# Latents normalised by token tile straight from PSUM, latent weights prepared in the first stage

## The chip, the cores and the metric

The kernel runs on one core of one Trainium2 chip. The metric is the device time of one execution in microseconds (us). On this core TensorE (PE) does the matrix products, VectorE (DVE), ScalarE (ACT) and GpSimd (POOL) work on tiles in the on-chip memory SBUF and, except POOL, in PSUM, where matmuls leave their sums; SyncE (SP) starts the transfers from HBM.

## The reference, cut to what matters

Two layers (DEPTH 2), 512 tokens, 1024 features. In each layer the normalised input is multiplied by one wide weight w_in, whose columns feed four head groups. The change is in the part that prepares group A, latent attention: two low-rank latents, cq (256 columns) and ckv (128 columns), are normalised and then multiplied by w_uq and w_ukv.

```python
for l in range(DEPTH):
    h = _rmsnorm(x, norm_g[l])
    p = _split(h @ w_in[l])
    o_a = _mla(p["a_cq"], p["a_ckv"], p["a_krope"], mla_qa_g[l], mla_w_uq[l],
               mla_kva_g[l], mla_w_ukv[l], cos, sin)
...
def _rmsnorm(x, g):
    xf = x.astype(jnp.float32)
    y = xf * lax.rsqrt(jnp.mean(xf * xf, axis=-1, keepdims=True) + NORM_EPS)
    return (y * g.astype(jnp.float32)).astype(x.dtype)
...
def _mla(cq, ckv, krope, qa_g, w_uq, kva_g, w_ukv, cos, sin):
    q = (_rmsnorm(cq, qa_g) @ w_uq).reshape(B, S, H, MLA_NOPE + MLA_ROPE)
    kv = (_rmsnorm(ckv, kva_g) @ w_ukv).reshape(B, S, H, MLA_NOPE + MLA_V)
    k_rope = _rope(krope, cos, sin)
    ...
```

The other head groups (differential, top-k selected and convolutional) follow in the same layer; the selected group needs 40 more columns (kidx and widx) that are produced together with the latents.

## The kernel before, in words

All matrix products are done on pairs of a rounded high part and the remainder: `mm3` issues three matmuls for one product (high by high, high by low, low by high). A weight tile arrives by DMA in a slot called wr, ACT casts it into wh (L106), and POOL subtracts (L101, 256 columns an instruction) to give wl. A result in PSUM is split by ACT (L115 or L118, the high part) and DVE (L116 or L119, the low part).

A Tile scheduler chooses the order of each engine's instructions from dependences and priorities, and every engine then works through its own list in that order: an instruction that waits holds up what stands behind it. Tiles come from pools with a fixed number of slots; a tile whose slots are all in use waits until one is freed. PSUM has eight banks: three called proj, two s, two pt, one o. Raw weights have four slots (wr), the split weights four each (wh, wl).

Each layer has a **first stage**: for four token tiles t and four quarters q of w_in's rows, `first_part` accumulates 456 columns in the PSUM tile acc[t] (cq 256, ckv 128, the rotary key krope 32, kidx and widx 40). The order over (t, q) is a written table, `FIRST`. The acc tiles of t = 0, 1 are proj banks, those of t = 2, 3 are s banks. With the last quarter ACT copies all 456 columns to SBUF (t1, L517).

Then follows the **latent stage**, `latent()`, on PE merged with 'features': `feat` projections of 128 columns of w_in for other groups (24 matmuls of 128x512 each, which need a proj bank, and whose result ACT and DVE evict). In program order the latent stage is:

- `rep`, a tile with kidx repeated (L587) and widx (L591), and `rep_turn`: four PE transposes of rep into a pt bank (L523), then kst (L594, L595);
- the sums of squares on ACT (L599, L600), one reciprocal root for all four token tiles and both latents (`rsqrt`, L140 to L147: a first guess from the bits and three Newton steps, 11 DVE instructions of 128x8), eight scalings to the tile cn (L608);
- twelve PE transposes of cn in three pt banks (L616), each split to cT (L118, L119);
- the rotary key: small DVE operations (L630 to L636), `rep_turn` again, and the split L640;
- w_ukv: DMA (L648), ACT cast (L651), two POOL subtractions (L654); then two key products, evicted by `halves`, and four value products (the `V` tiles), all in proj banks;
- w_uq: DMA (L671), eight casts on ACT (L681), eight subtractions on POOL (L682), four products.

Attention units (`unit_a`, L720) follow. Lines that the rows name besides: L186 to L199 is `params()`, once in the whole kernel, with one Exp table load on ACT (L197); L280 to L288 is the norm of whole rows of x, which uses a root on ACT (Sqrt), a DVE reciprocal and one Newton step; L217 builds a bias table.

## Time and profile before

| what | value |
|---|---|
| median of 3 runs | 704.25 us (703.63 to 704.76) |
| profiled execution | 706.75 us, its span 705.0 us |
| TensorE clock, mean granted | 0.969 |
| PE busy | 637.8 us (90%) |
| DVE busy | 490.3 us (70%) |
| ACT busy | 382.3 us (54%) |
| POOL busy | 275.7 us (39%) |

The time of a run is a little longer than the span from the first to the last instruction of the profile: 1.75 us in the profiled execution. Busy shares are averages over the span; the clock is the share of TensorE's full speed that was granted. "PEld" in the rows is PE's loading of weights, which lies beside its matmuls.

### The profile page before, as it was taken

To read this page: it belongs to the slowest core of one execution; us is meant where nothing else is said; L and a number is where in the kernel's file an instruction comes from. 1 tells how busy PE (TensorE), PEld (TensorE's weight loads), DVE (VectorE), ACT (ScalarE), POOL (GpSimd) and SP (SyncE) were. 2 spreads that over 40 slices of the span, in tenths; PEclk is the share of its full clock that TensorE was granted. 3 is DMA by queue.
4 is the path that set the end of the run, shared out by engine and by line. 5 is a ranking of instruction groups with operands and counts; after the bars stand their busy time and mean duration, and the time that the engine had idled before them with its cause. 6 is when DMAs were issued, how large, how long until landed. Compare 5 with 4: busy or idle time off the path is not lost. (4 is left out here: it accounts for less than half of the span.)

```text
span 705.0 us, 11082 instructions
## 1 busy us (share of the span) xinstructions
PE 637.8 (90%) x3600; PEld 538.9 (76%) x3608; DVE 490.3 (70%) x1464; ACT 382.3 (54%) x910; POOL 275.7 (39%) x408
## 2 busy tenths in 40 slices
PE   3987999789999898999999779998999999999994
PEld 2675878678788677899978567887878986789994
DVE  4665664389999797645384846769999959664537
ACT  7673475376453455454387355866554345445435
POOL 3173333413533443343432543234353354334355
PEclk9997999899999999999999889999999999999998
DMA  7545265384457220234261653354533841023203
GB/s 226 120 119 160 64 121 136 110 177 120 101 130 218 69 82 32 70 140 113 57 195 32 181 149 94 113 145 109 129 90 91 223 113 46 22 67 143 91 1 119
DMA packets 86441, 79.67 MB, mean 113 GB/s; under 512 B 7286, under 2 KB 73400, under 8 KB 86384
## 3 DMA queue, kind: packets, MB, share of 16 engines
q1 hardware_dynamic: 86384, 78.98, 40.7%
q8 instruction: 28, 0.46, 0.3%
q14 instruction: 29, 0.24, 0.1%
HBM read 64.18 MB, written 12.16 MB: 108 GB/s over the span
## 5 line engine op out<-in xcount | busy, mean ns | idle before, releaser
L101 POOL TENSOR_TENSOR wl<-wr,wh 128x256 fp32r<-128x256 f32 (+1 forms) x304 | 224.2, 770 | 355.6 <-ACT wh L106 287.1
L127 PE MATMUL ps_proj<-big,wh 128*128 128x512 f32 x768 | 257.3, 409 | 1.3 <-DVE prob L471 1.0
L127 PE MATMUL ps_proj<-wh,big 128*128 128x256 f32 (+2 forms) x768 | 173.8, 312 | 2.1 <-DVE prob L762 1.3
L127 PEld LDWEIGHTS ps_proj<-big,wh 128*128 128x128 f32 x768 | 142.2, 194 | 26.0 <-DVE prob L471 1.4
L127 PE MATMUL ps_proj<-big,wl 128*128 128x512 f32 x384 | 153.6, 400 | 0.0
L127 PEld LDWEIGHTS ps_proj<-wh,big 128*128 128x128 f32 x768 | 129.8, 193 | 8.5 <-ACT big L118 1.6
L127 PE MATMUL ps_proj<-wl,big 128*128 128x256 f32 (+2 forms) x384 | 117.4, 306 | 1.1 <-DVE wl L108 1.0
L106 ACT CAST wh<-wr 128x1024 fp32r<-128x1024 f32 (+2 forms) x84 | 83.8, 998 | 36.5 <-PE ps_proj L127 19.9
L127 PEld LDWEIGHTS ps_proj<-big,wl 128*128 128x128 f32 x384 | 73.8, 192 | 14.6
L127 PEld LDWEIGHTS ps_proj<-wl,big 128*128 128x128 f32 x384 | 74.3, 194 | 4.8 <-DVE wl L108 2.1
L116 DVE TENSOR_TENSOR ptl<-ps_pt,pth 128x128 fp32r<-128x128 f32 (+1 forms) x96 | 46.6, 485 | 33.5 <-ACT pth L115 32.9
L115 ACT CAST pth<-ps_pt 128x128 fp32r<-128x128 f32 (+1 forms) x96 | 40.6, 425 | 46.3 <-PE ps_pt L413 45.9
L127 PE MATMUL ps_o<-pth,vt 128*128 128x256 f32 (+1 forms) x288 | 60.9, 283 | 4.7 <-ACT pth L115 3.2
L477 ACT ACTIVATE prob<-ps_s,st_a 128x128 f32<-128x128 f32 (+1 forms) x64 | 33.9, 530 | 45.1 <-DVE st_a L489 29.6
L127 PEld LDWEIGHTS ps_o<-pth,vt 128*128 128x128 f32 x288 | 49.9, 198 | 9.8 <-ACT pth L115 6.3
L413 PE MATMUL ps_pt<-ident,prob 128*128 128x128 f32 x240 | 43.2, 279 | 11.6 <-ACT prob L481 8.9
L574 DVE MATCH_REPLACE8 ia<-m,ia 128x256 f32<-128x256 f32 (+2 forms) x96 | 52.0, 545 | 0.1
L573 DVE MAX8 m<-ia 128x8 f32<-128x256 f32 (+2 forms) x96 | 50.8, 551 | 1.0 <-POOL ia L565 0.8
L127 PE MATMUL ps_o<-ptl,vt 128*128 128x256 f32 (+1 forms) x144 | 42.8, 297 | 6.0 <-DVE ptl L116 6.0
L413 PEld LDWEIGHTS ps_pt<-ident,prob 128*128 128x128 f32 x240 | 28.5, 140 | 23.8 <-ACT prob L481 14.5
L481 ACT ACTIVATE prob<-prob,st_a 128x128 f32<-128x128 f32 (+1 forms) x64 | 35.8, 564 | 10.8 <-DVE st_a L480 10.7
L115 ACT CAST vt<-ps_proj 128x128 fp32r<-128x128 f32 x48 | 12.3, 265 | 46.8 <-PE ps_proj L127 29.1
(159 smaller groups left out, 1000.2 us busy)
## 6 DMA issues: line engine op xcount, KB each, us to landing
wr<-in_w_in_dram SPq DMA_DIRECT2D x56, 512.0 KB
big<-trip SPq DMA_DIRECT2D x64, 128.0 KB
trip<-big SPq DMA_DIRECT2D x28, 256.0 KB
big<-in_x_dram SPq DMA_DIRECT2D x7, 512.0 KB
wr<-in_w_in_dram SPq DMA_DIRECT2D x8, 416.0 KB
big<-trip SPq DMA_DIRECT2D x32, 96.0 KB
wr<-in_w_out_dram SPq DMA_DIRECT2D x8, 384.0 KB
big<-big SPq DMA_DIRECT2D x8, 256.0 KB
```

What stands on the lines that cost most here:

```text
L101: nc.gpsimd.tensor_tensor(out=o[:, c], in0=a[:, c], in1=b[:, c], op=OP.subtract)
L106: nc.scalar.copy(h[:, :n], raw[:, :n])
L115: nc.scalar.copy(hi, src)
L116: nc.vector.tensor_tensor(out=lo, in0=src, in1=f(hi), op=OP.subtract)
L127: nc.tensor.matmul(o, lhsT=a, rhs=b, start=start and i == 0 and j == 0, stop=stop and i == n - 1 and j == 2, skip_group_check=skip)
L413: nc.tensor.transpose(b[:, k * P:(k + 1) * P], p[:, k * P:(k + 1) * P], ident)
L477: nc.scalar.activation(p[:, :W], s[:, :W], AF.Exp, scale=-1.0, bias=mn, accum_out=sums)
L481: nc.scalar.activation(p[:, :W], p[:, :W], AF.Copy, scale=st[:, 2:3])
L573: nc.vector.max(out=m8, in_=a)
L574: nc.vector.match_replace(out=a, in_to_replace=m8, in_values=a, imm_value=MARK)
```

## The change

Two things change in each layer. First, each token tile is normalised on its own as soon as its last quarter is in PSUM (`first_norm`): ACT takes the squares from PSUM (with the 1/n as a scale), DVE adds the epsilon, ACT takes the root, DVE the reciprocal and one Newton step, and DVE scales from PSUM straight to cn. ACT copies only the 72 columns that are not latents to t1. The reciprocal root for all tiles together is gone, and with it the copy of 456 columns. What read t1 in two halves (rep, widx and the rotary key) now does so in one instruction for all four tiles. Second, the load and the split of w_ukv stand at the head of `latent()` (`latent_weights`) and no longer behind the rotary key. Lines below this point move by 7 to 20: L523 becomes L543, L616 L633, L651 L609, L654 L612, L681 L688.

```diff
--- before.py
+++ after.py
@@ -490,8 +490,9 @@
                                            scale=1.0, scalar=far, op0=OP.add, op1=OP.min, accum_out=mn)
 
 
-        t1s = [big(FT), big(FT)]
-        t1 = lambda t, c0, c1: t1s[t // 2][:, t % 2, c0:c1]
+
+        t1 = sm.tile([P, NT, 72], FT, name="t1", bufs=1)
+        cn = [flat(big(FT)), flat(big(FT))]
 
         acc, fw = {}, {}
 
@@ -514,7 +515,26 @@
             mm3(acc[t][:, :456], [hT.k(2 * q + k, t) + (wh[:, k, :], wl[:, k, :]) for k in range(2)],
                 start=q == 0, stop=q == 3)
             if q == 3:
-                nc.scalar.copy(t1(t, 0, 456), acc[t][:, :456])
+                first_norm(t, acc[t])
+
+        def first_norm(t, a):
+
+            w = sm.tile([P, 8], FT, name="ssa")
+            m, r, u = w[:, 0:2], w[:, 2:4], w[:, 4:6]
+            jk = prob()
+            for c, (c0, c1) in enumerate(((0, 256), (256, 384))):
+                nc.scalar.activation(jk[:, c0:c1], a[:, c0:c1], AF.Square, scale=(c1 - c0) ** -0.5,
+                                     accum_out=m[:, c:c + 1])
+            nc.vector.tensor_scalar(out=m, in0=m, scalar1=EPS, scalar2=None, op0=OP.add)
+            nc.scalar.activation(r, m, AF.Sqrt)
+            nc.scalar.copy(t1[:, t], a[:, 384:456])
+            nc.vector.reciprocal(out=r, in_=r)
+            nc.vector.tensor_tensor(out=u, in0=r, in1=r, op=OP.mult)
+            nc.vector.scalar_tensor_tensor(out=u, in0=u, scalar=-0.5, in1=m, op0=OP.mult, op1=OP.mult)
+            nc.vector.scalar_tensor_tensor(out=r, in0=u, scalar=1.5, in1=r, op0=OP.add, op1=OP.mult)
+            for c, (c0, c1) in enumerate(((0, 256), (256, 384))):
+                nc.vector.tensor_scalar(out=cn[t // 2][:, (t % 2) * 512 + c0:(t % 2) * 512 + c1], in0=a[:, c0:c1],
+                                        scalar1=r[:, c:c + 1], scalar2=None, op0=OP.mult)
 
         def rep_turn(rep):
 
@@ -580,33 +600,30 @@
 
 
 
+        def latent_weights():
+            raw = raw_tile()
+            nc.sync.dma_start(raw[:, :512], w_ukv[l])
+            w = big()
+            kh, kl = w[:, 0, :], w[:, 1, :]
+            rk = raw[:, :512].rearrange("p (h b c) -> p b h c", h=4, b=2)
+            nc.scalar.copy(kh.rearrange("p (b h c) -> p b h c", h=4, b=2), rk)
+            for b in range(2):
+                c = slice(b * 256, (b + 1) * 256)
+                nc.gpsimd.tensor_tensor(out=kl[:, c].rearrange("p (h c) -> p h c", h=4), in0=rk[:, b],
+                                        in1=f(kh)[:, c].rearrange("p (h c) -> p h c", h=4), op=OP.subtract)
+            A["ukv"] = kh, kl
+
         def latent():
+            latent_weights()
             rep = prob()
             repv = rep.rearrange("p (t r c) -> p t r c", t=NT, r=4)
-            for i in range(2):
-                nc.vector.tensor_copy(repv[:, 2 * i:2 * i + 2],
-                                      t1s[i][:, :, None, 416:448].to_broadcast([P, 2, 4, 32]))
+            nc.vector.tensor_copy(repv, t1[:, :, None, 32:64].to_broadcast([P, NT, 4, 32]))
             widx = A["widx"] = sm.tile([P, NT, 8], FT, name="widx", bufs=2)
-            for i in range(2):
-                nc.vector.tensor_copy(widx[:, 2 * i:2 * i + 2], t1s[i][:, :, 448:456])
+            nc.vector.tensor_copy(widx, t1[:, :, 64:72])
             b = rep_turn(rep)
             A["kst"] = kst = pi.tile([P, S], FR, name="kst")
             nc.scalar.copy(kst, b)
             nc.vector.tensor_tensor(out=kst[64:P], in0=b[64:P], in1=f(kst)[64:P], op=OP.subtract)
-            ss = sm.tile([P, NT, 2], FT, name="ssa")
-            for t in range(NT):
-                jk = prob()
-                nc.scalar.activation(jk[:, :256], t1(t, 0, 256), AF.Square, accum_out=ss[:, t, 0:1])
-                nc.scalar.activation(jk[:, 256:384], t1(t, 256, 384), AF.Square, accum_out=ss[:, t, 1:2])
-            for c, n in ((0, 256), (1, 128)):
-                nc.vector.tensor_scalar(out=ss[:, :, c], in0=ss[:, :, c], scalar1=1.0 / n, scalar2=EPS,
-                                        op0=OP.mult, op1=OP.add)
-            ra = rsqrt(ss.rearrange("p t c -> p (t c)"), 2 * NT)
-            cn = [flat(big(FT)), flat(big(FT))]
-            for t in range(NT):
-                for c, (c0, c1) in enumerate(((0, 256), (256, 384))):
-                    nc.vector.tensor_scalar(out=cn[t // 2][:, (t % 2) * 512 + c0:(t % 2) * 512 + c1], in0=t1(t, c0, c1),
-                                            scalar1=ra[:, 2 * t + c:2 * t + c + 1], scalar2=None, op0=OP.mult)
             yield CH[0]
             cT = []
             for j in (2, 0, 1):
@@ -623,14 +640,12 @@
             r2 = rep.rearrange("p (t r c) -> p t r c", t=NT, r=4)
             ta = sm.tile([P, NT, 16], FT, name="ropa", bufs=1)
             tb = sm.tile([P, NT, 16], FT, name="ropb", bufs=1)
-            for i in range(2):
-                x1, x2 = t1s[i][:, :, 384:400], t1s[i][:, :, 400:416]
-                tt = slice(2 * i, 2 * i + 2)
-                co, si = ctok[:, tt, 0:16], ctok[:, tt, 16:32]
-                nc.vector.tensor_tensor(out=ta[:, tt], in0=x2, in1=si, op=OP.mult)
-                nc.vector.tensor_tensor(out=tb[:, tt], in0=x1, in1=si, op=OP.mult)
-                nc.vector.tensor_tensor(out=r2[:, tt, 0, 0:16], in0=x1, in1=co, op=OP.mult)
-                nc.vector.tensor_tensor(out=r2[:, tt, 0, 16:32], in0=x2, in1=co, op=OP.mult)
+            x1, x2 = t1[:, :, 0:16], t1[:, :, 16:32]
+            co, si = ctok[:, :, 0:16], ctok[:, :, 16:32]
+            nc.vector.tensor_tensor(out=ta, in0=x2, in1=si, op=OP.mult)
+            nc.vector.tensor_tensor(out=tb, in0=x1, in1=si, op=OP.mult)
+            nc.vector.tensor_tensor(out=r2[:, :, 0, 0:16], in0=x1, in1=co, op=OP.mult)
+            nc.vector.tensor_tensor(out=r2[:, :, 0, 16:32], in0=x2, in1=co, op=OP.mult)
             nc.vector.tensor_tensor(out=r2[:, :, 0, 0:16], in0=r2[:, :, 0, 0:16], in1=ta, op=OP.subtract)
             nc.vector.tensor_tensor(out=r2[:, :, 0, 16:32], in0=r2[:, :, 0, 16:32], in1=tb, op=OP.add)
             nc.vector.tensor_copy(r2[:, :, 1:4, :], r2[:, :, 0:1, :].to_broadcast([P, NT, 3, 32]))
@@ -644,15 +659,7 @@
                 nc.sync.dma_start(f(kk)[96:100], dmask[:, 1])
             yield 0.4
 
-            raw = raw_tile()
-            nc.sync.dma_start(raw[:, :512], w_ukv[l])
-            kh, kl = (w[:, i, :] for w in (big(),) for i in range(2))
-            rk = raw[:, :512].rearrange("p (h b c) -> p b h c", h=4, b=2)
-            nc.scalar.copy(kh[:, :512].rearrange("p (b h c) -> p b h c", h=4, b=2), rk)
-            for b in range(2):
-                c = slice(b * 256, (b + 1) * 256)
-                nc.gpsimd.tensor_tensor(out=kl[:, c].rearrange("p (h c) -> p h c", h=4), in0=rk[:, b],
-                                        in1=f(kh)[:, c].rearrange("p (h c) -> p h c", h=4), op=OP.subtract)
+            kh, kl = A["ukv"]
             for j in range(2):
                 o = bank("proj")
                 mm3(o, [(kh[:, j * P:(j + 1) * P], kl[:, j * P:(j + 1) * P], ckv[:, 0, :], ckv[:, 1, :])])
```

The scheduler turns this into other lists. **PE, layer 0, end of the first stage**: `ps_s` is the last accumulation, L186 the transpose of parameters, `big,wh` and `big,wl` rows are a feature's matmuls. Before:

```order
L127 MATMUL ps_s<-wh,big 128x456
L186 MATMUL ps_pt<-ident,prow 128x20
L523 MATMUL ps_pt<-ident,prob 128x128 x2
L127 MATMUL ps_proj<-big,wh 128x512 x2
L127 MATMUL ps_proj<-big,wl 128x512
L127 MATMUL ps_proj<-big,wh 128x512 x2
L127 MATMUL ps_proj<-big,wl 128x512
L127 MATMUL ps_proj<-big,wh 128x512
L523 MATMUL ps_pt<-ident,prob 128x128 x2
L127 MATMUL ps_proj<-big,wh 128x512
L127 MATMUL ps_proj<-big,wl 128x512
```

After:

```order
L127 MATMUL ps_s<-wh,big 128x456
L186 MATMUL ps_pt<-ident,prow 128x20
L127 MATMUL ps_proj<-big,wh 128x512 x2
L127 MATMUL ps_proj<-big,wl 128x512
L127 MATMUL ps_proj<-big,wh 128x512 x2
L127 MATMUL ps_proj<-big,wl 128x512
L127 MATMUL ps_proj<-big,wh 128x512 x2
L543 MATMUL ps_pt<-ident,prob 128x128 x4
L127 MATMUL ps_proj<-big,wl 128x512
L127 MATMUL ps_proj<-big,wh 128x512 x2
```

The transposes of rep stood in two pairs, the first directly behind L186 and the second five feature matmuls later; now all four stand together, behind eight feature matmuls.

**ACT, layer 0, latent stage**: `wh<-wr` are weight casts, L118 and L115 are evictions from PSUM, the L517, L599 and L600 rows above these are gone. Before, from the cast of kst:

```order
L594 CAST kst<-ps_pt 128x512
L600 ACTIVATE prob,ssa<-big 128x128
L599 ACTIVATE prob,ssa<-big 128x256
L600 ACTIVATE prob,ssa<-big 128x128
L106 CAST wh<-wr 128x1024 x2
L118 ACTIVATE big<-ps_proj 128x512
L118 ACTIVATE big<-ps_pt,pcol 128x512 x3
L115 CAST big<-ps_pt 32x1024
L106 CAST wh<-wr 128x1024
L651 CAST big<-wr 128x512
L118 ACTIVATE big<-ps_proj 128x512
L681 CAST big<-wr 128x256 x2
```

After, from the last tile's surroundings:

```order
L106 CAST wh<-wr 128x1024
L529 ACTIVATE ssa<-ssa 128x2
L609 CAST big<-wr 128x512
L625 CAST kst<-ps_pt 128x512
L106 CAST wh<-wr 128x1024
L118 ACTIVATE big<-ps_proj 128x512
L118 ACTIVATE big<-ps_pt,pcol 128x512 x3
L115 CAST big<-ps_pt 32x1024
L115 CAST big<-ps_proj 64x512
L106 CAST wh<-wr 128x1024
L115 CAST big<-ps_proj 64x512
L197 ACT_TABLE_LOAD
```

The cast of w_ukv (L651, now L609) moved from behind the evictions of cT to a place ahead of kst; the root of the last tile (L529) stands behind a weight cast; and the table load of `params()` (L197), which stood in the first stage, now stands among the evictions of the key products.

**ACT, layer 1, end of the first stage.** Before:

```order
L517 COPY big<-ps_s 128x456
L599 ACTIVATE prob,ssa<-big 128x256
L600 ACTIVATE prob,ssa<-big 128x128
L106 CAST wh<-wr 128x1024
L517 COPY big<-ps_s 128x456
L599 ACTIVATE prob,ssa<-big 128x256
L600 ACTIVATE prob,ssa<-big 128x128
L594 CAST kst<-ps_pt 128x512
L106 CAST wh<-wr 128x1024 x2
L118 ACTIVATE big<-ps_proj 128x512
L118 ACTIVATE big<-ps_pt,pcol 128x512 x3
```

After:

```order
L530 COPY t_4180<-ps_s 128x72
L529 ACTIVATE ssa<-ssa 128x2
L106 CAST wh<-wr 128x1024
L609 CAST big<-wr 128x512
L526 ACTIVATE prob,ssa<-ps_s 128x256
L526 ACTIVATE prob,ssa<-ps_s 128x128
L530 COPY t_4180<-ps_s 128x72
L529 ACTIVATE ssa<-ssa 128x2
L106 CAST wh<-wr 128x1024
L625 CAST kst<-ps_pt 128x512
L106 CAST wh<-wr 128x1024
L118 ACTIVATE big<-ps_proj 128x512
```

A weight cast now stands between the last tile's root and the cast of kst (L594, now L625), where kst stood ahead of both casts before.

## Rows read from the trace of the kernel before

**Rows 1.** The page's first part: busy us (share of the span) xinstructions

```profile
PE 637.8 (90%) x3600; PEld 538.9 (76%) x3608; DVE 490.3 (70%) x1464; ACT 382.3 (54%) x910; POOL 275.7 (39%) x408
```

**Rows 2.** Timeline of PE, layer 0: start, us, line, count [idle before <-releaser]

```profile
42.38 0.37 PE L127 MATMUL ps_s<-wh,big 128*128 128x456 f32 x1
...
54.96 1.12 PE L616 MATMUL ps_pt<-ident,big 128*128 128x128 f32 x4 [3.99 <-DVE big L608]
...
60.08 0.39 PE L127 MATMUL ps_proj<-big,wl 128*128 128x512 f32 x1
...
60.31 0.39 PE L127 MATMUL ps_proj<-big,wh 128*128 128x512 f32 x1
...
64.91 0.73 PE L127 MATMUL ps_proj<-big 128*128 128x512 f32 x2 [0.72 <-ACT big L651]
...
67.93 2.08 PE L127 MATMUL ps_proj<-big 128*128 128x512 f32 x4 [2.29 <-POOL big L654]
...
70.66 0.63 PE L127 MATMUL ps_proj<-big,wl 128*128 128x512 f32 x1
...
73.64 0.64 PE L127 MATMUL ps_proj<-big,wh 128*128 128x512 f32 x2
```

**Rows 3.** Timeline of PE, layer 1

```profile
397.61 0.33 PE L616 MATMUL ps_pt<-ident,big 128*128 128x128 f32 x1 [2.88 <-DVE big L608]
...
399.00 0.47 PE L616 MATMUL ps_pt<-ident,big 128*128 128x128 f32 x1 [1.06 <-DVE big L608]
...
400.41 1.79 PE L616 MATMUL ps_pt<-ident,big 128*128 128x128 f32 x6 [0.94 <-DVE big L608]
...
404.79 0.48 PE L127 MATMUL ps_proj<-big,wl 128*128 128x512 f32 x1
...
409.94 0.73 PE L127 MATMUL ps_proj<-big 128*128 128x512 f32 x2 [1.46 <-ACT big L651]
...
412.96 2.08 PE L127 MATMUL ps_proj<-big 128*128 128x512 f32 x4 [2.29 <-POOL big L654]
...
418.55 0.63 PE L127 MATMUL ps_proj<-big,wh 128*128 128x512 f32 x2
```

**Rows 4.** Windows: stretch, length, busy PE, PEld, DVE, ACT, POOL, PEclk, DMA

```profile
54.96:74.12 19.16, 16.15 (x53) 11.97 (x54) 8.98 (x17) 8.92 (x19) 7.59 (x14) 0.69 0.45 127
606.00:609.60 3.60, 3.53 (x14) 3.33 (x15) 0.38 (x3) 0.00 (x0) 0.00 (x0) 0.53 0.32 106
238.70:242.00 3.30, 3.07 (x16) 2.36 (x17) 2.21 (x9) 2.11 (x6) 0.21 (x1) 1.00 0.88 242
```

**Rows 5.** Timeline of DVE, layer 0 and then layer 1

```profile
49.15 0.66 DVE L145 TENSOR_TENSOR rs_t<-rs_y 128x8 f32<-128x8 f32 x1
...
53.95 0.17 DVE L146 SCALAR_TENSOR_TENSOR rs_t<-rs_t,ssa 128x8 f32<-128x8 f32 x1
...
396.58 4.23 DVE L608 TENSOR_SCALAR big<-big,rs_y 128x256 f32<-128x256 f32 x8
```

**Rows 6.** Timeline of POOL, layer 0

```profile
35.64 8.46 POOL L101 TENSOR_TENSOR wl<-wr,wh 128x256 fp32r<-128x256 f32 x12 [11.06 <-ACT wh L106]
48.35 5.54 POOL L101 TENSOR_TENSOR wl<-wr,wh 128x256 fp32r<-128x256 f32 x8 [4.26 <-ACT wh L106]
```

**Rows 7.** Timeline of ACT, layer 0

```profile
40.75 0.42 ACT L599 ACTIVATE prob<-big 128x256 f32<-128x256 f32 x1
...
42.11 1.28 ACT L197 ACT_TABLE_LOAD   x1
```

**Rows 8.** Groups by line and shape, ACT: busy us, mean ns

```profile
L280 ACT ACTIVATE nw<-ss 128x1 f32<-128x1 f32 x12 | 3.5, 288 | 0.1
```

**Rows 9.** Timeline of ACT, layer 1

```profile
396.24 1.04 ACT L106 CAST wh<-wr 128x1024 fp32r<-128x1024 f32 x1 [1.88 <-DMA wr<-in_w_in_dram]
```

**Rows 10.** Timeline of PE, two later waits

```profile
238.84 0.39 PE L752 MATMUL ps_s<-big 128*128 128x256 f32 x1 [2.15 <-DVE prob L762]
...
606.07 0.55 PE L127 MATMUL ps_o<-ptl,vt 128*128 128x256 f32 x1 [1.63 <-DVE ptl L116]
```

## The prediction

> **What bounds the kernel now.** I read the page first: PE is busy for 637.8 us, 90% of the span [rows 1], so what can be gained lies in the places where PE waits or runs slowly. The timeline of PE shows these around the change. In layer 0 the first stage's last matmul starts at 42.38 and ends at 42.75. Then PE stands still three times: 3.99 us before the transposes of cn, released by a scaling L608 on DVE; 0.72 before the key products, released by the cast L651; 2.29 before the next product, released by POOL's subtraction L654 [rows 2]. Layer 1 has the same three places: 2.88, 1.06 and 0.94 behind L608, 1.46 behind L651, 2.29 behind L654 [rows 3]. Sums: 7.00 and 8.63.
>
> After long waits the matmuls themselves are slower. A 128x512 matmul is followed by the next after 0.23 us at 60.08, but seven of them take 2.98 from 70.66 to 73.64, 0.43 each [rows 2]. The windows view says why: over 54.96 to 74.12 the granted clock was 0.69, and where a stretch is slow from end to end it is 0.53, the lower level of 1.2 GHz, against 1.00 at 2.4 GHz [rows 4]. In the timeline the slow stretches last from 54.96 to 60.08 and from 67.93 to 73.64, in layer 1 from 400.41 to 404.79 and from 412.96 to 418.55 [rows 2, 3]: 5.12, 5.71, 4.38 and 5.59 us. At half speed half of each is lost: 2.56, 2.86, 2.19, 2.80, together 10.4. What the two stages lose is thus 7.00 + 8.63 + 10.4 = 26.0 us.
>
> Who sets the long wait? The root of all tiles is one chain of dependent DVE instructions of 128x8. Beside POOL's subtractions they take 0.66 each, and 0.17 as soon as POOL has stopped (it worked from 48.35 to 53.89) [rows 5, 6]. The later waits are only a matter of place: w_ukv is split when ACT and POOL come to it.
>
> **The change part by part.**
>
> *The waits for L651 and L654.* The cast of w_ukv now stands ahead of kst on ACT, and POOL's two pieces follow it. They are over before the cn transposes start, since ACT has the one cast and POOL two pieces of about 0.7 (5.54 for 8) [rows 6] to do. Both waits go: 0.72 + 2.29 and 1.46 + 2.29, with the slow stretches behind them.
>
> *The wait for L608.* PE has feature matmuls from the last accumulation up to the cn transposes, before and after; it came there at 50.97 (54.96 - 3.99) [rows 2]. In the new order tiles 0 and 1 are scaled by about 46. Tile 3 is last: its root stands behind a cast of 1.04 [rows 9], then come reciprocal, three Newton operations and two scalings. If POOL subtracts meanwhile, three operations of 0.66 (2.0) instead of 0.17 (0.5) [rows 5]. I come to 52.3 to 53.2 for the last scaling. PE, which loses some time ahead of this (next part), comes there at 52.6 to 53.1. I put the wait at 0, with 1.0 as the upper bound. In layer 1 tiles 0 to 2 are finished inside the first stage, but a weight cast has moved ahead of what PE needs, and this cast can start only when its DMA has landed: at 396.24 in the trace, after 1.88 of waiting [rows 9]. From this I work out 2.75 us of waiting at the cn transposes of layer 1, between 0 and 3.9 (the sum of the last two waits there now, 1.06 + 0.94, and another 1.9).
>
> A rule of the Trainium skill speaks against small chains here: "SBUF — State Buffer", section "Who interferes with whom", says that DVE and POOL share one port pair as an exclusive lock, which a DVE instruction with two SBUF inputs needs, while one with at most one SBUF input outside certain fast modes doesn't. The 0.66 against 0.17 agree [rows 5]. By that rule the new scalings, which read PSUM, are free of POOL, whereas the scalings from SBUF took 0.53 each beside it (4.23 for 8) [rows 5]; no row here has a scaling from PSUM. Counted at 0.53 the eight cost 4.2 a layer on DVE, at an estimated 0.35 they cost 2.8; DVE has room for either except for tile 3's two, 0.4 us, which lies inside the bound of 1.0.
>
> *A new wait at the first transposes of rep (L543).* Before, half of rep was transposed early, half five matmuls later. Now all four transposes need the 72 columns of all four tiles, and behind them in PE's list stand all the feature matmuls and the cn transposes. PE gets there eight matmuls after the stage, 42.9 + 8 x 0.23 = 44.75 [rows 2]. ACT does per tile two squares, the small copy and a root of 0.29 [rows 8]. From a first square at 40.75 to the table load at 42.11, 1.36 us [rows 7], lie one such pair and one copy of 456 columns; with a copy of 72 I estimate 1.05 (0.8 and 0.25). All of it is in one queue in which a root waits for DVE's add, and that add stands on DVE behind the Newton operations of the tile before, at 0.66 each until POOL stops at 44.10 [rows 5, 6]. By this the last small copy ends at 46.3, the 512-column copy of rep on DVE 0.5 to 0.7 later, and the transposes start at 47.4: a wait of 2.6 us, with bounds of 0.9 (ACT never held up: 42.75 + 0.8 + 0.25 + 0.7 and the queue's steps, 45.65) and 3.5. In layer 1, where three tiles are done earlier, 0.9, between 0.3 and 1.5.
>
> *What was hidden under the removed waits.* Between the first cn transpose and the first value product, 54.96 to 74.12, PE has 19.16 - 0.72 - 2.29 - 5.42 = 10.7 us of work at full clock, and ACT was busy for 8.92 [rows 4]. Of this the cast L651 goes (about 0.6), and in layer 0 the table load (1.28 [rows 7]) with its two exponentials comes in: 10.0. The two engines are now of nearly the same length and take turns: an eviction on ACT waits for PE's product, a proj bank for the eviction, and behind the evictions stand the casts for the next features. Neither hides the other fully. Going through both lists row by row I get a wait of 1.3 at the third feature and 2.45 at the value products in layer 0, and 1.85 and 1.35 in layer 1 (no table load, but the late cast). Bounds: nothing, and 6 in each layer.
>
> *What costs nothing.* Fewer, larger rotary instructions; and the smaller copy, 72 instead of 456 columns. Holding the acc banks up to the scaling costs nothing in layer 0: the features that take these proj banks come 5 us later. The number of table loads stays the same.
>
> *The clock.* Whether a new wait brings the clock down isn't clear from its length: after 2.15 us at 238.84 the window is at 1.00, after 1.63 at 606.07 it is at 0.53 [rows 4, 10]. I count one fall per layer, 2.6 each (the mean of the four above, 10.4 / 4); bounds are none and two.
>
> **The sum.** New waits in layer 0: 2.6 + 0 + 1.3 + 2.45 = 6.35. In layer 1: 0.9 + 2.75 + 1.85 + 1.35 = 6.85. Clock 5.2. Gain: 26.0 - 6.35 - 6.85 - 5.2 = 7.6 us. The lists of PE behind the latent stage hold the same work, and PE is the engine that is short there, so I let the gain stand to the end. The profiled execution of 706.75 (span 705.0) would become 699.15. It is 2.5 above the median of 704.25; taken from the median, 696.6.
>
> **The rivals.**
>
> *The new waits are small (gain 13 to 21).* If ACT keeps up with PE, the waits at the proj banks go, and the clock holds. For it: ACT stood idle for over half of the stretch [rows 4], and each wait is then under 3 us. Against it: ACT's gaps are waits for PE, not room. Time with only the waits of rep and of layer 1's transposes left: 704.25 - (26.0 - 2.6 - 0.9 - 2.75) = 684.5.
>
> *The clock falls at every new wait (gain about 2).* Two falls per layer as now: 26.0 - 13.2 - 10.4 = 2.4, so 701.9. For it: a fall after 1.63 [rows 10]. Against it: the new waits are split in smaller pieces with matmuls in between.
>
> *Slower: a convoy on ACT.* A weight cast needs a free slot, which PE frees only after a whole feature, 24 x 0.23 = 5.5 us. If an eviction stands right behind such a cast and PE, further on, waits for the bank of that eviction, PE loses up to 5.5 in each layer more than counted: 13.2 + 5.2 + 11 = 29.4 against 26.0, hence 3.4 slower, 707.6. It decides from 3.8 us more per layer. For it: in both layers the first key eviction stands directly ahead of a weight cast and the others behind it. Against it: the slots are four, and now too the cast at 396.24 waited for its DMA and not for a slot [rows 9].
>
> *Nothing is left of it.* The gain at the start is given back at some later stage that DVE sets (the top-k search) or that waits for a DMA: 704. Against it: DVE's work moves forward with PE's.
>
> **How the numbers follow.** The forecast (gain 4 to 13, 691 to 700) has 0.50. Small new waits (under 691) 0.16. Clock falls everywhere (700 to 703) 0.16. No change left 0.08, the convoy 0.10. A measurement of this kernel tells a difference of about 0.2% (1.4 us) from none. Faster takes the forecast, the first rival and most of the second: 0.79. Within 0.2%: 0.10, slower 0.11. The range goes from 686, into the first rival, to 704, past the second: outside lie about 0.08 below and 0.12 above. The forecast's own range is 691 to 700.
>
> **What would show it.** Right: no wait with L612 or L609 as the releaser; at the cn transposes (L633) under 1 us in layer 0; a new wait of 2 to 3.5 at L543 in layer 0; small waits released by ACT or DVE at products in proj banks; PE's first score (L727) about 3 to 5 us earlier in layer 0, about 8 earlier relative to before in layer 1. Wrong: a wait at L543 of 4 or more, waits at the proj banks of over 6 per layer, or a first score earlier by the same amount as I say and an end that isn't.

## The result, and the profile after

The changed kernel took 680.61 us (680.28 to 680.91, 4 runs) against 704.5 us: a ratio of 0.966, with a 95% interval of 0.965 to 0.968. That is 23.9 us less, three times the 7.6 that were forecast, and below the range. The profiled execution took 680.28 us.

The page's busy times and TensorE's clock in 40 slices (tenths of full speed):

```profile
PE 623.6 (92%) x3600; PEld 529.5 (78%) x3608; DVE 489.9 (72%) x1466; ACT 378.1 (56%) x918; POOL 277.1 (41%) x408
...
PEclk9999999799999999999999999999999999999998
```

PE is busy for 14.2 us less than in [rows 1] with as many instructions: more of the same matmuls ran at the higher clock.

The timeline of PE of the changed kernel, at the places of [rows 2] and [rows 3] and at the new waits:

```profile
41.83 0.37 PE L127 MATMUL ps_s<-wh,big 128*128 128x456 f32 x1
...
43.09 0.69 PE L127 MATMUL ps_proj<-big,wh 128*128 128x512 f32 x2 [0.73 <-DVE big L536]
...
46.03 0.66 PE L543 MATMUL ps_pt<-ident,prob 128*128 128x128 f32 x4 [0.87 <-DVE prob L620]
...
51.54 1.03 PE L633 MATMUL ps_pt<-ident,big 128*128 128x128 f32 x8
...
61.18 0.88 PE L127 MATMUL ps_proj<-big 128*128 128x256 f32 x6
...
378.68 0.66 PE L543 MATMUL ps_pt<-ident,prob 128*128 128x128 f32 x4 [1.37 <-DVE prob L620]
...
383.76 0.73 PE L127 MATMUL ps_proj<-big,wh 128*128 128x512 f32 x2 [0.79 <-DVE kst L626]
...
385.25 1.03 PE L633 MATMUL ps_pt<-ident,big 128*128 128x128 f32 x8
...
395.69 0.98 PE L127 MATMUL ps_proj<-big 128*128 128x256 f32 x6 [1.62 <-DVE big L119]
```

All waits of [rows 2] and [rows 3] are gone: nothing waits for a scaling at the cn transposes (L633), and none is released by the cast or the subtraction of w_ukv. New are 0.73 and 0.87 in layer 0, 1.37, 0.79 and 1.62 in layer 1: 5.4 us in all, where 13.2 were forecast. The windows between the first cn transpose and the first value product, and three more, as in [rows 4]:

```profile
51.54:61.18 9.64, 9.64 (x50) 7.31 (x48) 6.40 (x13) 6.74 (x11) 4.60 (x7) 1.00 0.80 235
385.25:395.69 10.44, 8.82 (x48) 7.11 (x46) 6.67 (x10) 8.62 (x14) 5.51 (x8) 1.00 0.83 240
...
120.00:130.00 10.00, 6.53 (x33) 6.00 (x34) 4.18 (x6) 3.51 (x7) 5.58 (x8) 0.66 0.49 149
140.00:150.00 10.00, 8.61 (x60) 7.63 (x60) 9.58 (x26) 8.42 (x23) 1.42 (x2) 1.00 0.35 87
...
580.00:590.00 10.00, 8.91 (x53) 7.48 (x52) 6.11 (x21) 4.60 (x13) 1.92 (x3) 1.00 0.12 39
```

The stretch that took 19.16 us in [rows 4] takes 9.64 in layer 0, at a clock of 1.00, and PE is busy without a gap.

The sum: 26.0 us of waits and slow stretches removed, 5.4 of new waits, and 0.37 that the second half of the rep transposes had waited before: 21.0. The last matmul of the first stage starts 0.55 earlier (41.83 against 42.38; why, no row says), and a later slow stretch is gone. The wait of 1.63 at 606.07 [rows 10] is one of 1.09 in the changed kernel, at 581.41, and the clock behind it is 1.00 (the last window above); the window of before was

```profile
600.00:610.00 10.00, 8.29 (x38) 6.51 (x37) 6.23 (x21) 3.70 (x9) 3.64 (x6) 0.83 0.12 39
```

At 0.83 a third of the ten us was at the lower clock, 3.4, and half of that, 1.7, was lost. Together 23.3, beside the 23.9 of the medians.

These rows of before, however, are those of an execution of 706.75 us, so the two profiles lie 26.5 apart, and 3.2 of that is not in the sum. The first transposes of the attention stage in each layer, before (two rows) and after, tell where:

```profile
94.10 0.33 PE L413 MATMUL ps_pt<-ident,prob 128*128 128x128 f32 x1 [1.40 <-ACT prob L481]
...
439.29 0.33 PE L413 MATMUL ps_pt<-ident,prob 128*128 128x128 f32 x1 [1.70 <-ACT prob L481]
```

```profile
82.06 0.33 PE L413 MATMUL ps_pt<-ident,prob 128*128 128x128 f32 x1 [1.17 <-ACT prob L481]
...
416.66 0.33 PE L413 MATMUL ps_pt<-ident,prob 128*128 128x128 f32 x1 [1.17 <-ACT prob L481]
```

They run 12.0 and 22.6 us earlier. Without the 0.55 that is 22.1 for the two stages, where the sum has 21.0; 0.8 of the difference is in the waits at these transposes themselves. The remaining 3.9 come behind them in layer 1: the slow stretch of 1.7, and 2.2 that I did not trace.

### The profile page after: what moved, and what is told of

Read it like the earlier page. It is cut to its first block, busy times and chain, and to the rows that moved or that the text cites. A ratio compares the mean times of both kernels' runs of the same rounds, so it can differ in the third digit from the quotient of the medians.

```text
span 678.5 us, 11101 instructions
## 1 busy us (share of the span) xinstructions
PE 623.6 (92%) x3600; PEld 529.5 (78%) x3608; DVE 489.9 (72%) x1466; ACT 378.1 (56%) x918; POOL 277.1 (41%) x408
## 4 chain that ended last, share of the span: by engine, by line
PE 58%; DVE 27%; ACT 8%; DMA 3%; issue 2%; POOL 1%; SPq 0%; DVEq 0%; ACTq 0%; POOLq 0%
PE ps_proj L127 43%; DVE ia L594 5%; PE ps_o L127 5%; DVE m L593 4%; PE ps_pt L413 3%; PE ps_s L127 2%; DVE big L119 2%; DVE ptl L116 2%; ACT wh L106 1%; ACT prob L477 1%; DVE ps_s L489 1%; DMA wr<-in_w_in_dram 1%; ACT prob L575 1%; ACT prob L481 1%; DVE ia L580 1%
## 5 line engine op out<-in xcount | busy, mean ns | idle before, releaser
L127 PE MATMUL ps_proj<-big,wh 128*128 128x512 f32 x768 | 250.6, 401 | 2.8 <-DVE prob L471 1.0
L127 PEld LDWEIGHTS ps_proj<-big,wh 128*128 128x128 f32 x768 | 138.7, 189 | 27.6 <-DVE prob L471 1.4
L127 PE MATMUL ps_proj<-big,wl 128*128 128x512 f32 x384 | 151.8, 395 | 0.0
L127 PEld LDWEIGHTS ps_proj<-big,wl 128*128 128x128 f32 x384 | 72.3, 188 | 14.2
L115 ACT CAST pth<-ps_pt 128x128 fp32r<-128x128 f32 (+1 forms) x96 | 40.5, 425 | 43.8 <-PE ps_pt L413 43.4
L594 DVE MATCH_REPLACE8 ia<-m,ia 128x256 f32<-128x256 f32 (+2 forms) x96 | 52.0, 544 | 0.2
L413 PEld LDWEIGHTS ps_pt<-ident,prob 128*128 128x128 f32 x240 | 28.5, 140 | 23.3 <-ACT prob L481 12.6
L580 DVE SCALAR_TENSOR_TENSOR ia<-prob,widx,ia 128x256 f32<-128x256 f32 (+2 forms) x42 | 26.2, 640 | 12.7 <-ACT prob L575 12.0
```

What stands on the lines that cost most here:

```text
L115: nc.scalar.copy(hi, src)
L127: nc.tensor.matmul(o, lhsT=a, rhs=b, start=start and i == 0 and j == 0, stop=stop and i == n - 1 and j == 2, skip_group_check=skip)
L413: nc.tensor.transpose(b[:, k * P:(k + 1) * P], p[:, k * P:(k + 1) * P], ident)
L580: nc.vector.scalar_tensor_tensor(out=a, in0=r[:, :W], scalar=w, in1=a, op0=OP.mult, op1=OP.add)
L594: nc.vector.match_replace(out=a, in_to_replace=m8, in_values=a, imm_value=MARK)
```

## The experiments

Two theories stood against each other at first. **Own price**: each removed wait gives back its own length and the slow stretch behind it. **Takes turns** (the step of the prediction on PE and ACT): a removed wait comes back in part at the proj banks. A second pair, **short** and **early**, is about what in the new norm does the work. Times are medians; each run of a group shares its runs of the kernel before (704.7, 705.2 and 704.2 us). The changed kernel itself was run again only in the third group (after_again).

### One part alone: w_only and n_only

`w_only` is the kernel before with the split of w_ukv at the head of `latent()`:

```diff
         def latent():
+            latent_weights()
             rep = prob()
...
+            kh, kl = A["ukv"]
```

> Only the early split of w_ukv, the latents normalised as before. If the waits are independent (theory 'own price'), the waits for L651 and L654 and the slow stretches behind them go and nothing else: 0.72 + 2.29 + 2.86 and 1.46 + 2.29 + 2.80 = 12.4 us, so about 692 us, and the waits for the scaling stay at about 4.0 in layer 0 and 4.9 in layer 1. If the waits take each other's place (theory 'takes turns', the step of the prediction on ScalarE and TensorE), a good part of the 12.4 comes back at products in proj banks: 696 us or more.

`n_only` is the changed kernel with that call back behind the rotary key:

```diff
         def latent():
-            latent_weights()
...
+            latent_weights()
             kh, kl = A["ukv"]
```

> Only the normalisation by token tile, the split of w_ukv where it was. 'Own price': the waits for L608 and their slow stretches go, 3.99 + 2.56 and 4.88 + 2.19 = 13.6, less the waits that the changed kernel shows at the first transposes of rep (0.87 and 1.37) and the two beside them (0.73, 0.79): about 10 us, 694 us; the waits for the cast and for POOL's subtraction stay at 2 to 4 us a layer. 'Takes turns': the stretch behind, now reached earlier by TensorE but not by ScalarE and GpSimd, waits longer there, so the gain is under 6 us: 698 us or more.

Measured: w_only 692.34 us (ratio 0.982, 0.979 to 0.985), n_only 693.95 us (0.985, 0.981 to 0.989). That is 12.3 and 10.7 less than before; "own price" had said 12.4 and 10. Their sum, 23.0, is nearly the whole 23.9, though the intervals leave each of the two uncertain by 2 to 3 us. The waits of PE in w_only (first two rows) and in n_only:

```profile
54.28 0.59 PE L630 MATMUL ps_pt<-ident,big 128*128 128x128 f32 x3 [2.72 <-DVE big L622]
...
394.55 2.71 PE L630 MATMUL ps_pt<-ident,big 128*128 128x128 f32 x8 [4.81 <-DVE big L622]
```

```profile
60.52 2.93 PE L127 MATMUL ps_proj<-big 128*128 128x512 f32 x6 [2.95 <-ACT big L609]
...
398.22 0.73 PE L127 MATMUL ps_proj<-big 128*128 128x512 f32 x2 [1.46 <-ACT big L609]
...
401.24 1.80 PE L127 MATMUL ps_proj<-big 128*128 128x512 f32 x4 [2.28 <-POOL big L612]
```

Each part leaves the other's waits where they were: 2.72 and 4.81 for the scaling (3.99 and 4.88 before), 2.95 and 3.74 for w_ukv (3.01 and 3.75 before). Only the first is clearly shorter, by 1.3. So the two parts hardly touch each other. w_only also had small waits of 0.6 to 1.2 at value products, n_only waits of 0.73 and 0.86 in layer 0 and one of 1.86 at the rep transposes of layer 1, after which the clock fell (0.83 over 380 to 390 us).

### More work on ACT: uq_twice and ev_twice

`uq_twice` makes each cast of w_uq twice, `ev_twice` each cast that evicts a key product (the second cast writes the same values).

```diff
                     nc.scalar.copy(dv, src)
+                    nc.scalar.copy(dv, src)
```

> The changed kernel with each of the eight casts of w_uq on ScalarE made twice, 1.7 us more on ScalarE in each layer between the evictions of the key products and those of the value products. 'Takes turns': TensorE loses it in both layers, 3.4 us, 684 us. Rival 'slack' (three proj banks and the feature matmuls between let TensorE run ahead of ScalarE): nothing in layer 0, where the changed kernel shows no wait in this stretch, and up to 1.7 in layer 1, where it shows one of 1.62 behind ScalarE's evictions: 680.6 to 682.3 us.

```diff
-                halves(A["k"][j], o)
+                (hi, lo), s = A["k"][j], o
+                for i in range(2):
+                    nc.scalar.copy(hi[0:64, i, :], s[64 * i:64 * i + 64])
+                    nc.scalar.copy(hi[0:64, i, :], s[64 * i:64 * i + 64])
+                    nc.vector.tensor_tensor(out=lo[0:64, i, :], in0=s[64 * i:64 * i + 64], ...)
```

> The changed kernel with each of the four evicting casts of the key products on ScalarE made twice: 0.58 us more each, 2.3 us more on ScalarE in each layer, this time directly on the way from a product to the release of its proj bank. 'Takes turns': all of it is lost, 4.6 us, 685 us. 'Slack': in layer 0, where the changed kernel shows no wait here, TensorE waits under 1 us; in layer 1, where it waits 1.62 already, 1 to 2.3 more: 681.5 to 684 us in all.

Measured: uq_twice 681.14 us (0.967, 0.964 to 0.970), no different from the changed kernel. Its profile reached the stage 1.3 earlier and lost as much to a fall of the clock at 220 to 230 us (0.83). From the first feature of layer 0 on, the stage took 0.4 longer (to the transpose of 82.06, here at 81.23), in layer 1 nothing, with the wait of 1.62 as before. The scheduler put the second casts partly between and behind the value evictions, so this shows room behind the evictions of the key products, not ahead of them. ev_twice is the harder test, and took 687.95 us (0.976, 0.973 to 0.979), more than either theory said. Its rows in the stretch, and two windows:

```profile
60.81 0.88 PE L127 MATMUL ps_proj<-big 128*128 128x256 f32 x6
...
63.95 0.60 PE L127 MATMUL ps_proj<-big 128*128 128x256 f32 x3 [0.52 <-DVE big L670]
...
66.58 2.71 PE L127 MATMUL ps_proj<-big 128*128 128x512 f32 x10 [0.29 <-POOL big L693]
...
83.32 0.33 PE L413 MATMUL ps_pt<-ident,prob 128*128 128x128 f32 x1 [1.16 <-ACT prob L481]
...
401.54 1.39 PE L127 MATMUL ps_proj<-big 128*128 128x256 f32 x6 [2.98 <-DVE big L119]
```

```profile
397.50:405.00 7.50, 4.52 (x17) 3.54 (x16) 3.93 (x8) 6.58 (x20) 6.18 (x12) 0.79 0.56 148
140.00:150.00 10.00, 8.60 (x37) 7.28 (x37) 8.36 (x22) 9.03 (x24) 1.42 (x2) 0.66 0.26 64
```

In layer 0 the first value product ran 0.4 earlier than in the changed kernel (60.81 against 61.18) and the transpose behind the stage 1.3 later (83.32 against 82.06). So 2.3 us more on ACT cost 1.6, more than the waits of 0.52 and 0.29 show: the slack was 0.7 us. In layer 1 the wait of 1.62 grew to 2.98, 1.4 of the 2.3, and the clock fell (0.79; 3.2 us slow, 1.6 lost). That makes 4.6 in the two stretches: as a sum what "takes turns" had said, but in part by the clock. The rest is elsewhere: from 140 to 150 us the clock was 0.66, where the changed kernel has 1.00, and from 230 to 240 it was 0.83. By PE's rows the attention stage of layer 0 took 2.3 us longer for the first (55.84 for 53.51 between the rows that start at 120.68 and 174.19 in the changed kernel), and a later stretch 1.3 for the second, although the edit touches neither. These 8.2 are above the 7.6 between the two profiles, since ev_twice came to the stage 0.4 earlier and gained 0.4 between the layers.

### What in the norm does it: n_long and n_batch

`n_long` keeps the tiles apart but takes the old root of eleven instructions for each. `n_batch` is w_only with the short root for all tiles in one batch.

```diff
-            nc.scalar.activation(r, m, AF.Sqrt)
...
+            r = rsqrt(m, 2)
```

> The changed kernel with the old eleven-instruction root, now of 128x2 for each token tile, in place of ScalarE's root, the reciprocal and one Newton step: 24 more small VectorE instructions per layer and no root on ScalarE. If the wait went because each tile starts as soon as it is ready ('early'), the time stays within 2 us of 680.6. If it went because the chain is shorter ('short'), the last tile's chain of nine operations with two inputs beside GpSimd's subtractions (about 0.66 each, some 6 us instead of 2) comes too late for the transposes: a wait of 3 to 5 us and a slow stretch in each layer, 690 us or more.

```diff
-            ra = rsqrt(ss.rearrange("p t c -> p (t c)"), 2 * NT)
+            nc.scalar.activation(ra, v, AF.Sqrt)
+            nc.vector.reciprocal(out=ra, in_=ra)
+            nc.vector.tensor_tensor(out=u, in0=ra, in1=ra, op=OP.mult)
+            nc.vector.scalar_tensor_tensor(out=u, in0=u, scalar=-0.5, in1=v, op0=OP.mult, op1=OP.mult)
+            nc.vector.scalar_tensor_tensor(out=ra, in0=u, scalar=1.5, in1=ra, op0=OP.add, op1=OP.mult)
```

> Early w_ukv as in the run with that part alone (692.3 us), the latents still in one batch from copies in SBUF, but with ScalarE's root, a reciprocal and one Newton step of 128x8 in place of eleven instructions; one more table load (1.28 us) in layer 0. 'Short' alone: the chain is shorter by 5 to 6 operations of 0.66 or 0.17, so the waits of 2.72 and 4.81 at the cn transposes shrink to about 1 and 2, and the slow stretches go: 685 us. 'Early' (each tile as soon as it is ready) is needed too: the batch starts only after the last squares, the waits stay at 2 to 4 us: 690 us or more.

Measured: n_long 692.53 us (0.982, 0.978 to 0.985), n_batch 694.54 us (0.985, 0.982 to 0.987). The waits of PE in n_long:

```profile
45.59 1.19 PE L127 MATMUL ps_proj<-big,wh 128*128 128x512 f32 x2 [3.27 <-DVE ssa L528]
...
386.70 1.11 PE L539 MATMUL ps_pt<-ident,prob 128*128 128x128 f32 x4 [5.37 <-DVE prob L616]
...
404.85 0.70 PE L127 MATMUL ps_proj<-big,wh 128*128 128x512 f32 x2 [2.44 <-DVE big L116]
```

The size was as "short" had said, the place was not. The long chains are in time for the cn transposes, but DVE's list is so full of them that the first feature matmul waits 3.27 (its row in the changed kernel: 0.73, released by a scaling out of the first stage's bank; here too the scalings from a proj bank ended at 45.36, just before the add that the row names) and the copy of rep comes 5.37 late. n_batch:

```profile
63.30 0.75 PE L127 MATMUL ps_proj<-big,wh 128*128 128x512 f32 x2 [3.76 <-DVE big L119]
...
391.85 0.48 PE L637 MATMUL ps_pt<-ident,big 128*128 128x128 f32 x1 [2.63 <-DVE big L629]
```

Its cn transposes wait 0.83 in layer 0 and 2.63 + 0.94 in layer 1, less than w_only's 2.72 and 4.81; but another wait of 3.76 appears in layer 0 behind the evictions, in a kernel with one more table load ahead of the scalings (at 49.80), and nothing is gained over w_only. Neither the short root alone nor the early start alone brings the gain. That both are needed is shown for the early start only in part: 4.4 us of waiting stay at the cn transposes in n_batch, but its load and its wait of 3.76 are not separated from the batch.

### The waits that are left: eps_bias, rep_halves, uq_early, rep_psum, rep_eps

```diff
-            nc.vector.tensor_scalar(out=m, in0=m, scalar1=EPS, scalar2=None, op0=OP.add)
-            nc.scalar.activation(r, m, AF.Sqrt)
+            nc.scalar.activation(r, m, AF.Sqrt, bias=epsc)
+            nc.vector.tensor_scalar(out=m, in0=m, scalar1=EPS, scalar2=None, op0=OP.add)
```

> The changed kernel with the epsilon as the root's bias on ScalarE, so that the root waits for no VectorE add (the add is made beside it, for the Newton step). If ScalarE's waits for that add (0.70 and 2.03 in layer 0, 0.40 and 1.07 in layer 1) are what holds the last small copy and the copy of rep ('round trip'), the wait at the first transposes of rep goes from 0.87 and 1.37 to under 0.5 each and the wait behind kst in layer 1 (0.79) goes as well: 2 to 3 us less, 678 us. If rep waits for VectorE alone (its copies and chains beside GpSimd's subtractions), nothing changes by more than 1 us.

```diff
-            nc.vector.tensor_copy(repv, t1[:, :, None, 32:64].to_broadcast([P, NT, 4, 32]))
+            for i in range(2):
+                nc.vector.tensor_copy(repv[:, 2 * i:2 * i + 2],
+                                      t1[:, 2 * i:2 * i + 2, None, 32:64].to_broadcast([P, 2, 4, 32]))
```

> The changed kernel with the copy of rep in two halves, as before the change. The scheduler places two transposes three feature matmuls later. If the one copy of 512 columns (0.42 in layer 0, 1.02 beside GpSimd in layer 1) is what the transposes wait for, the waits of 0.87 and 1.37 fall by about half: 1 us less, 679.5 us. If the last token tile's small copy is, nothing changes: 680.6 us.

In eps_bias, epsc is a column that holds EPS. For `uq_early` the block that loads and splits w_uq moves, as a function, to the place behind kst:

```diff
             nc.vector.tensor_tensor(out=kst[64:P], in0=b[64:P], in1=f(kst)[64:P], op=OP.subtract)
+            uq_weights()
```

> The changed kernel with the split of w_uq moved up as well, behind kst: eight casts (1.7 us) leave ScalarE's list among the evictions, and eight subtractions of GpSimd come earlier. 'Takes turns': 3 us less, 677.5 us. 'Slack': the wait of 1.62 in layer 1 goes only if ScalarE's length is its cause; it is released by an eviction that stands ahead of the casts, so no change in layer 0 and under 1 us in layer 1, against 1 to 2 us lost where VectorE's chains now lie beside more of GpSimd's subtractions: 680 to 682 us.

```diff
             nc.scalar.copy(t1[:, t], a[:, 384:456])
+            nc.scalar.copy(rep0[:, t * P:(t + 1) * P].rearrange("p (r c) -> p r c", r=4),
+                           a[:, None, 416:448].to_broadcast([P, 4, 32]))
...
-            nc.vector.tensor_copy(repv, t1[:, :, None, 32:64].to_broadcast([P, NT, 4, 32]))
```

> The changed kernel with rep written by ScalarE straight from PSUM, tile by tile (four more copies of 128 columns per layer, about 0.25 us each), and the copy of rep on VectorE left away. If the transposes of rep wait for VectorE's copy beside GpSimd's subtractions, the waits of 0.87 and 1.37 go; in layer 1 kst then stands ahead of the weight casts that wait for their DMA and 0.79 goes as well: 2 to 3 us less, 678 us. If ScalarE's queue is the limit (its waits for the add of the epsilon, 2.03 and 1.07), the waits stay at the first three transposes, which now stand directly behind the first stage: no change or 1 us more.

The tile rep0 takes the place of rep. `rep_eps` has the edits of eps_bias and rep_psum; `after_again` is the changed kernel beside them.

> Both: rep from PSUM by ScalarE, and the epsilon as the root's bias, so that ScalarE waits neither for VectorE nor VectorE's copy stands between. All waits at the first transposes of rep and behind kst go, 0.87 + 1.37 + 0.79, less 0.5 for what ScalarE's own work still takes: 678 us; 681 or more only if the clock falls once more in the attention stage than in the changed kernel, which the windows of 120 to 150 us would show.

> The changed kernel as it is, beside the next three on one chip: 680.6 us again, with waits of 0.73 and 0.87 in layer 0 and 1.37, 0.79 and 1.62 in layer 1.

Measured: eps_bias 684.33 us (0.970), rep_halves 682.13 (0.969), uq_early 684.78 (0.972, 0.969 to 0.976); then after_again 680.03 (0.965, 0.963 to 0.967), rep_psum 679.92 (0.965), rep_eps 679.38 (0.964, 0.962 to 0.967). None is clearly better than the changed kernel, and eps_bias and uq_early are 3.7 and 4.2 us above its 680.6. Three of PE's waits: in eps_bias, uq_early and rep_eps:

```profile
383.23 0.69 PE L545 MATMUL ps_pt<-ident,prob 128*128 128x128 f32 x4 [2.29 <-DVE prob L622]
```

```profile
47.13 0.65 PE L543 MATMUL ps_pt<-ident,prob 128*128 128x128 f32 x4 [2.87 <-DVE prob L636]
```

```profile
382.51 0.73 PE L127 MATMUL ps_proj<-big,wh 128*128 128x512 f32 x2 [2.27 <-DVE kst L628]
```

In eps_bias the wait behind kst is gone, but rep comes later (2.29 for 1.37): the last small copy on ACT ended at 380.34, and DVE came to the copy of rep only at 382.31. DVE is the engine that is late there, not ACT. In rep_halves the first half waits as well (0.94 and 1.72), so the length of that copy isn't the cause. rep_eps, which takes DVE out of rep's way, has only 0.28 of waiting left in layer 0 and none at rep in layer 1, but 2.27 behind kst in place of 1.37 + 0.79 (1.37 + 0.67 in after_again); rep_psum has 1.56 at rep in layer 0 and 2.20 behind kst. In layer 1 the wait only moves: DVE finishes tile 3's chain and then kst, and a feature matmul waits for that. Why this matmul depends on kst's instruction I could not settle. uq_early puts 2.87 at rep in layer 0, for 0.87. It didn't touch the wait of 1.62 either (1.55): so the casts are not its cause; it is released by an eviction.

## Why the prediction was wrong

*The removed waits and slow stretches: right.* The 26.0 us are 12.4 and 13.6 for the two parts; w_only gave 12.3, n_only 10.7 with 3.45 of waits of its own (0.73, 0.86 and 1.86).

*"Neither hides the other fully": the step that failed.* It counted 1.3 + 2.45 in layer 0 and 1.85 + 1.35 in layer 1; measured were 0 and 1.62, so 5.3 us too much. From nearly equal lengths, 10.7 and 10.0 us, I concluded that PE and ACT take turns. But what counted here is what stands ahead of what on ACT. The casts of w_uq stand behind the evictions that PE needs next, and while the table load holds up an eviction PE has another bank and feature matmuls to go on with. The changed kernel's ACT at that place:

```profile
59.11 0.57 ACT L115 CAST big<-ps_proj 64x512 fp32r<-64x512 f32 x1
59.70 1.28 ACT L197 ACT_TABLE_LOAD   x1
...
62.90 1.68 ACT L688 CAST big<-wr 128x256 fp32r<-128x256 f32 x8
64.49 0.42 ACT L115 CAST vt<-ps_proj 128x128 fp32r<-128x128 f32 x2
```

The first value products run at 61.18, before these casts begin at 62.90. The two runs with more work on ACT bear this out: 1.7 us more behind the evictions of the key products cost 0.4 and 0, and 2.3 more ahead of them cost 1.6 and 1.4 of waiting. They also show that it was close, since the slack in layer 0 was only 0.7 us.

*The clock: one fall per layer counted, none came.* 5.2 us of the miss. In the two stages the new waits are 1.62 and less, and the windows show 1.00.

*The cn transposes: right in layer 0 (no wait), wrong in layer 1.* There 2.75 were counted for a weight cast that waits for its DMA. It did wait, 3.10 us, and the cast of kst stood behind it, but PE had features to do; what was left is 0.79.

```profile
381.02 1.06 ACT L106 CAST wh<-wr 128x1024 fp32r<-128x1024 f32 x1 [3.10 <-DMA wr<-in_w_in_dram]
```

*The wait at the rep transposes: right in place, too long in layer 0, too short in layer 1.* 2.6 and 0.9 counted; 0.87 and 1.37 measured. In layer 0 ACT's last small copy started at 44.93 and took 0.22, so it ended at 45.15 and not 46.3. The transposes ran at 46.03 and not 47.4, and PE came there 0.4 later (45.16) because of a wait that I had excluded: "Holding the acc banks up to the scaling costs nothing" was false, since the first feature waited 0.73 for it; n_long makes that 3.27.

*The port lock.* The trace after bears on what no row had shown, a scaling from PSUM beside POOL. DVE and then POOL, layer 1:

```profile
375.63 0.66 DVE L534 SCALAR_TENSOR_TENSOR ssa<-ssa 128x2 f32<-128x2 f32 x1
376.40 0.74 DVE L536 TENSOR_SCALAR big<-ps_s,ssa 128x256 f32<-128x256 f32 x2
```

```profile
371.36 7.85 POOL L101 TENSOR_TENSOR wl<-wr,wh 128x256 fp32r<-128x256 f32 x11 [15.05 <-ACT wh L106]
```

Two scalings in layer 0 while POOL stood still (from 43.45 to 46.18), and the eight scalings from SBUF of the kernel before in layer 0, when POOL had stopped:

```profile
44.61 0.74 DVE L536 TENSOR_SCALAR big<-ps_proj,ssa 128x256 f32<-128x256 f32 x2
```

```profile
54.35 1.93 DVE L608 TENSOR_SCALAR big<-big,rs_y 128x256 f32<-128x256 f32 x8
```

Both of a tile's scalings take 0.74 together, 0.37 each, whether POOL subtracts or not, whereas the Newton step ahead of them takes 0.66 beside POOL. The Trainium skill, "SBUF — State Buffer", section "Who interferes with whom", says so: with at most one SBUF input and outside the fast modes a DVE instruction doesn't contend with POOL. The lower of my two prices, 0.35, was the right one. From SBUF a scaling took 0.24 in the mean without POOL and 0.53 beside it [rows 5], so reading PSUM saves time only where POOL is at work.

In sum, by the medians: 7.8 too much for the new waits (13.2 for 5.4; 5.3 of it the failed step), 5.2 for the clock, 3.3 in things not counted (0.37, 0.55, 1.7 and a rest of 0.7, which is 3.2 between the two profiles). Of the rivals the first, small new waits with the clock held, is what happened; its 684.5 was still 3.9 too high.

## What to carry to other kernels

A wait on the engine that bounds the kernel is worth its length plus the slow stretch behind it, and two such waits can simply add, as they did here within what the runs can tell. Before assuming that a removed wait comes back, look at what stands in the other engine's list between the last eviction the bounding engine needs and the next: here work behind that point cost at most a quarter of its length, work ahead of it about two thirds, and the equal lengths alone did not tell which. A short chain did not pay here without its early start, nor the early start with a long chain, since each early chain adds its small instructions to a list that others wait for.

## What the runs showed of the hardware

The length of a wait alone doesn't decide whether the clock falls. The same wait and the next one behind it, in the changed kernel and in uq_twice:

```profile
226.43 0.39 PE L759 MATMUL ps_s<-big 128*128 128x256 f32 x1 [2.16 <-DVE prob L769]
...
240.13 0.39 PE L127 MATMUL ps_o<-ptl,vt 128*128 128x256 f32 x1 [0.86 <-DVE ptl L116]
```

```profile
225.31 0.39 PE L760 MATMUL ps_s<-big 128*128 128x256 f32 x1 [2.16 <-DVE prob L770]
...
240.31 0.39 PE L127 MATMUL ps_o<-ptl,vt 128*128 128x256 f32 x1 [0.86 <-DVE ptl L116]
```

The wait is 2.16 both times, but from the one row to the other it is 13.70 us at a clock of 1.00, and 15.00 in uq_twice, where the window of 220 to 230 us shows 0.83. Behind kst in layer 1 the clock fell after a wait of 2.20 in rep_psum (0.83 over 380 to 390 us) and not after 2.27 in rep_eps (1.00). After the waits of 1.62 to 1.64 in the latent stage of layer 1 it stayed up in every run that had one, but in the kernel before it fell after 1.63 at 606.07 [rows 10], and in n_only after 1.86.

Such falls come and go far from the edit. In the attention stage of layer 0, which no experiment touches, the changed kernel and all its variants have a slow stretch between 120 and 140 us (0.66 over 120 to 130 in the changed one). ev_twice, eps_bias and uq_early have a second one from 140 to 150 us (0.66, 0.66 and 0.70, where the changed kernel has 1.00), and PE's rows put its price at 2.1 to 2.3 us. With the 1.3 of the wait above that is 3.5 of the 5.2 us by which the profile of eps_bias ends later than that of the changed kernel, more than the last edits could bring. Executions of one kernel differ in the same way: the four of eps_bias took 681.65 to 685.75 us at mean clocks of 0.99 to 0.98, and its profile is of the longest. So of kernels a few us apart the profile has to say whether the edit or the clock made the difference.
